# An encoder layer in split float32r: a quarter of the low parts made by an adding transfer instead of VectorE

## The chip, the cores and the metric

The kernel runs on one core of one Trainium2 chip. The metric is the device time of one execution in microseconds (us), the median of several runs. The engines are named as the profile names them: PE (TensorE), PEld (its weight loads), DVE (VectorE), ACT (ScalarE), POOL (GpSimd) and SP (SyncE, which here only issues transfers).

## What is computed

One encoder layer on 256 tokens of width 2048, all in float32:

```python
x = x + 0.5 * swiglu(rms_norm(x, ffn1_norm), ffn1_w_gu, ffn1_w_down)    # 2048 -> 2 x 5632 -> 2048
h = rms_norm(x, mix_norm); p = h @ w_in                                 # 2048 -> 4608
x = x + concat(gqa_axial(p), diff_attention(p)) @ w_out                 # 8 + 4 heads, 256 x 256 scores
x = x + 0.5 * swiglu(rms_norm(x, ffn2_norm), ffn2_w_gu, ffn2_w_down)
x = rms_norm(x, out_norm)
```

Nearly all of the arithmetic is in the products with the weights, about 338 MB of them, each read once from HBM.

## The kernel before

Tokens lie on the partitions of every result. To get float32 accuracy from float32r products, each operand is split into a high part (a cast to float32r) and a low part (the operand minus its high part), and each product is three matmuls: high x high, high x low, low x high (lines 191, 192 and 193). The high part of a weight is made by ACT (line 125, tile `whi`), the low part by DVE (line 126, tile `wlo`), both from the loaded tile `raw`.

`mm_block` is the loop around every weight product. It works on a block of up to 1024 columns of the weights and walks down its rows in **steps**. A step c takes 256 rows, that is two row blocks of 128, k = 2c and 2c + 1. One transfer issued by SP loads both (line 172, 1024 KB, into one of three `raw` buffers), ACT casts the two row blocks, DVE makes the two low parts, and PE runs 2 banks x 2 token tiles x 2 row blocks x 3 = 24 matmuls of 128 x 512. `whi` and `wlo` have four buffers each, which is two steps' worth. The last step of a block is followed by an evacuation on DVE or ACT.

Three stages follow each other: the first feed-forward half step (about 0 to 730 us), the mixer (about 730 to 1050 us) and the second feed-forward half step. In the mixer DVE has more to do beside the low parts: QK norms (`ssq`, line 406), rotary, the 32 x 32 transposes of the heads (`kTa`, `qT`, `kTb`, line 432) and the softmax (`mx`, `nb`, `ri`, `e`, lines 452 to 488). POOL computes a part of the rotary there (`tmp`, line 421) and the reciprocal roots (`rs`, line 100). In the very first block of the kernel x and x.T are loaded beside the weights (`x`, `raw_x`), and the first two steps are loaded in quarters (line 169). In the very last block, `t_major`, the work is ordered by token tile.

The order of the instructions on each engine is chosen by a scheduler at build time, which goes by its own simulated times; a tile pool makes the writer of a buffer wait for that buffer's readers. So the raw buffer of step c takes the load of step c + 3, and SP waits for the last reader of it.

Of the kernel before, what the change touches and what calls it, by code (L numbers as in the profile page):

```python
# [13 lines left out]
F32 = mybir.dt.float32  # L14
F32R = mybir.dt.float32r
AF = mybir.ActivationFunctionType
ALU = mybir.AluOpType
# [24 lines left out]
def encoder_layer(ctx: ExitStack, tc: tile.TileContext, a: dict, out: bass.AP):  # L42
    """Tokens lie on the partitions of x and of every product's result; the operands of the weight
    products are split into two float32r parts that add up to them exactly, and each product runs as
    hi*hi + hi*lo + lo*hi on the tensor engine."""
# [5 lines left out]
    wlo_p = ctx.enter_context(tc.tile_pool(name="wlo", bufs=4))  # L51
# [14 lines left out]
    def load_gain(n):  # L66
        """a norm's gain with the features on partitions, [128, 16]"""
        g = const.tile([P, NK], F32, name=f"gain_{n}")
        nc.gpsimd.dma_start(g, a[n])
        return g  # L70
# [3 lines left out]
    # The tensor engine's clock rises while the first loads are under way.  # L74
# [6 lines left out]
    # Stages of side work (transposes, attention) wait here, to be issued between the steps of a  # L81
    # weight product once their operands are long there.
# [13 lines left out]
    def rsqrt_mean(dst, ssq, n, width):  # L96
        """dst = (ssq / n + EPS) ** -0.5"""
# [6 lines left out]
    class Norm:  # L104
        """rstd of x, gathered by pieces of the columns, in their order."""
# [21 lines left out]

    def new_xT():
        return (xt_p.tile([P, NK, T], F32R, name="xT_hi"), xt_p.tile([P, NK, T], F32R, name="xT_lo"))

    def fill_xT(xT, g, ks):
        """xT[:, k, :] = (x * gain).T for two k at a time."""
# [16 lines left out]
    def late_load(dst, src):  # L149
        """a load for later, kept from running ahead of the first weights"""  # L150
# [3 lines left out]
    def mm_block(lhs, nk, w, row0, col0, width, evac, before=None, after=None, slots=1, t_major=None):  # L154
        """out[t][:, b * 512:...] = lhs.T @ w[row0:row0 + nk * 128, col0:col0 + width], by banks."""
# [4 lines left out]
        parts = {}  # L160

        def load(c):
# [12 lines left out]
            for j in range(2):  # L175
                own = t_major is not None and c > 0
                hi = (t_major if own else whi_p).tile([P, WB], F32R, name="whi")
                lo = (t_major if own else wlo_p).tile([P, WB], F32R, name="wlo")
                for b in range(0, width, fine):
                    splits.append(split(hi[:, b:b + fine], lo[:, b:b + fine], raw[:, j, b:b + fine]))  # L180
                parts[2 * c + j] = (hi, lo)

        def mm(b, t, ks, c0=0, c1=512):
            if ks[0] == 0:
                ps[b, t] = ps_mm.tile([P, 512], F32, name="psm")
            o = ps[b, t][:, c0:c1]
            for k in ks:
# [3 lines left out]
                nc.tensor.matmul(o, xh, wh, start=k == 0, stop=False)  # L191
                nc.tensor.matmul(o, xh, wl, start=False, stop=False)  # L192
                nc.tensor.matmul(o, xl, wh, start=False, stop=k == nk - 1)  # L193
# [478 lines left out]
```

## Time and profile before

| what | value |
|---|---|
| median of 3 runs | 1803.1 us (1802.27 to 1803.56) |
| span of the profiled execution | 1797.4 us, 5.7 us below the median; the page lists no other time for it |
| PE busy | 1772.5 us (99% of the span), 7860 matmuls |
| DVE busy | 1191.6 us (66%) |
| ACT busy | 808.2 us (45%) |
| POOL busy | 47.3 us (3%) |
| DMA | 341.03 MB, mean 190 GB/s; SP's queue 56.4% of 16 engines' span |
| granted PE clock | 0.998 of full speed, mean |

The span runs from the first to the last instruction. An engine's busy share is a mean over the three stages. A wait is put down to what came last before the waiting engine went on. DMA share is the mean busy share of the core's 16 DMA engines.

### The profile page before, as it was taken

What the parts mean: (1) busy time and instruction counts of PE and PEld (TensorE: products, weight loads), DVE (VectorE), ACT (ScalarE), POOL (GpSimd) and SP (SyncE); (2) the same over time, 40 slices, a digit from 0 to 9 for tenths busy, and PEclk for the clock granted to TensorE, in tenths of its full rate; (3) what the DMA queues carried; (4) which work ended last, traced back from release to release, by engine and by line L of the source; (5) the groups of instructions that cost most, each with busy time, mean ns of one, the idle gap of its engine ahead of it and who ended that gap; (6) DMA issues with size and microseconds to landing.
All of it is one profiled execution on the core that took longest, in us unless ns stands there. A gap on an engine that the chain in (4) does not pass through costs nothing.

```text
span 1797.4 us, 20551 instructions
## 1 busy us (share of the span) xinstructions
PE 1772.5 (99%) x7860; PEld 1462.0 (81%) x7860; DVE 1191.6 (66%) x1763; ACT 808.2 (45%) x1073; POOL 47.3 (3%) x75
## 2 busy tenths in 40 slices
PE   9999999999999999998999999999999999999998
PEld 7888888888888888877778888888888888888886
DVE  6475855845846767779987664566746746647676
ACT  6444443443443444745555354343443443443444
POOL 0000000000000000112110000000000000000000
PEclk9999999999999999999999999999999999999999
DMA  9555565565655475654345455565555555655573
GB/s 344 195 187 190 186 210 188 187 200 190 197 191 198 148 234 184 195 184 163 113 146 188 166 185 187 191 206 188 189 193 200 190 190 195 201 187 188 154 242 120
DMA packets 97667, 341.03 MB, mean 190 GB/s; under 512 B 6384, under 2 KB 7840, under 8 KB 97440
## 3 DMA queue, kind: packets, MB, share of 16 engines
q1 hardware_dynamic: 96752, 338.39, 56.4%
q8 instruction: 61, 1.00, 0.2%
q10 hardware_dynamic: 720, 1.31, 0.2%
q14 instruction: 38, 0.31, 0.1%
q0 software_dynamic: 96, 0.02, 0.0%
HBM read 337.60 MB, written 2.10 MB: 189 GB/s over the span
## 4 chain that ended last, share of the span: by engine, by line
PE 91%; DVE 6%; issue 1%; DMA 1%; ACT 1%; POOL 0%; POOLq 0%; ACTq 0%
PE psm L192 30%; PE psm L193 30%; PE psm L191 30%; DVE wlo L126 2%; DVE qT L432 1%; DVE kTb L432 1%; POOL tmp L421 0%; PE psx L138 0%; DMA raw<-in_ffn_w_down 0%; PE psx L535 0%; PE psx L515 0%; DVE kTa L432 0%; DVE ssq L406 0%; PE psx L500 0%; DVE tmp L414 0%
## 5 line engine op out<-in xcount | busy, mean ns | idle before, releaser
L126 DVE TENSOR_TENSOR wlo<-raw,whi 128x1024 fp32r<-128x1024 f32 (+1 forms) x676 | 758.4, 1152 | 550.7 <-ACT whi L125 546.6
L125 ACT CAST whi<-raw 128x1024 fp32r<-128x1024 f32 (+1 forms) x676 | 649.4, 996 | 842.4 <-PE psm L193 750.9
L192 PE MATMUL psm<-wlo,xT_hi 128*128 128x512 f32 x1696 | 659.9, 392 | 8.7 <-DVE wlo L126 8.5
L193 PE MATMUL psm<-whi,xT_lo 128*128 128x512 f32 x1696 | 657.3, 390 | 0.0
L191 PE MATMUL psm<-whi,xT_hi 128*128 128x512 f32 x1696 | 585.9, 390 | 1.4 <-ACT xT_hi L317 1.4
L192 PEld LDWEIGHTS psm<-wlo,xT_hi 128*128 128x128 f32 x1696 | 318.7, 188 | 78.2 <-DVE wlo L126 12.4
L191 PEld LDWEIGHTS psm<-whi,xT_hi 128*128 128x128 f32 x1696 | 318.3, 188 | 68.4 <-ACT xT_hi L317 2.3
L193 PEld LDWEIGHTS psm<-whi,xT_lo 128*128 128x128 f32 x1696 | 318.8, 188 | 65.7
L192 PE MATMUL psm<-wlo,hT_hi 128*128 128x512 f32 x836 | 323.1, 389 | 0.0
L193 PE MATMUL psm<-whi,hT_lo 128*128 128x512 f32 x836 | 322.8, 389 | 0.0
L191 PE MATMUL psm<-whi,hT_hi 128*128 128x512 f32 x836 | 295.2, 389 | 0.0
L192 PEld LDWEIGHTS psm<-wlo,hT_hi 128*128 128x128 f32 x836 | 157.0, 188 | 32.4 <-DVE wlo L126 0.4
L193 PEld LDWEIGHTS psm<-whi,hT_lo 128*128 128x128 f32 x836 | 157.0, 188 | 32.1
L191 PEld LDWEIGHTS psm<-whi,hT_hi 128*128 128x128 f32 x836 | 157.0, 188 | 32.1
L270 DVE STREAM_TRANSPOSE turned<-h 32x256 f32<-32x256 f32 (+1 forms) x384 | 158.8, 413 | 6.5
L228 DVE SCALAR_TENSOR_TENSOR x<-psm,x 128x512 f32<-128x512 f32 (+1 forms) x113 | 72.1, 679 | 5.7 <-PE psm L193 5.2
L122 POOL TENSOR_TENSOR rstd<-ms,minus_half 128x1 f32<-128x1 f32 x8 | 4.6, 575 | 1498.7 <-DVE ms L121 1498.7
L125 ACT CAST hT_hi<-turned 128x512 fp32r<-128x512 f32 x44 | 24.1, 617 | 38.5 <-DVE turned L270 38.5
L432 DVE STREAM_TRANSPOSE qT<-tmp 32x128 f32<-32x128 f32 x128 | 38.7, 302 | 1.7
L242 ACT ACTIVATE sg<-psm,rstd 128x512 f32<-128x512 f32 x44 | 28.4, 687 | 9.5 <-PE psm L193 9.5
L257 DVE SCALAR_TENSOR_TENSOR h<-psm,rstd,sg 128x512 f32<-128x512 f32 x44 | 32.0, 747 | 0.3
L126 DVE TENSOR_TENSOR hT_lo<-turned,hT_hi 128x512 fp32r<-128x512 f32 x44 | 30.0, 686 | 1.4 <-ACT hT_hi L125 1.4
(94 smaller groups left out, 400.7 us busy)
## 6 DMA issues: line engine op xcount, KB each, us to landing
raw<-in_ffn_w_gu SPq DMA_DIRECT2D x158, 1024.0 KB, 4.9
raw<-in_ffn_w_down SPq DMA_DIRECT2D x88, 1024.0 KB, 5.0
raw<-in_w_in SPq DMA_DIRECT2D x32, 1024.0 KB, 5.1
raw<-in_ffn_w_gu SPq DMA_DIRECT2D x32, 512.0 KB, 3.7
raw<-in_w_out SPq DMA_DIRECT2D x16, 1024.0 KB, 4.9
raw<-in_w_in SPq DMA_DIRECT2D x8, 512.0 KB, 3.8
raw<-in_ffn_w_gu SPq DMA_DIRECT2D x8, 256.0 KB, 5.3
x<-in_x SPq DMA_DIRECT2D x8, 256.0 KB, 9.6
```

The lines of the kernel that those rows point to most:

```text
L122: nc.gpsimd.tensor_tensor(self.rstd[t], ms, minus_half[:, :1], op=ALU.pow)
L125: nc.scalar.copy(hi, src)
L126: return nc.vector.tensor_tensor(lo, src, f32(hi), op=ALU.subtract)
L191: nc.tensor.matmul(o, xh, wh, start=k == 0, stop=False)
L192: nc.tensor.matmul(o, xh, wl, start=False, stop=False)
L193: nc.tensor.matmul(o, xl, wh, start=False, stop=k == nk - 1)
L228: nc.vector.scalar_tensor_tensor(x[t][:, s], ps[:, c0:c1], scale, x[t][:, s], op0=ALU.mult, op1=ALU.add)
L242: nc.scalar.activation(sg[t][:, b * 512:(b + 1) * 512], ps, AF.Silu, scale=norm.rstd[t][:, 0:1])
L257: nc.vector.scalar_tensor_tensor(h[t][:, s], ps, norm.rstd[t][:, 0:1], sg[t][:, s], op0=ALU.mult, op1=ALU.mult)
L270: nc.vector.transpose(turned[q * B32:(q + 1) * B32, :nk, t * P + i * B32:t * P + (i + 1) * B32], src[:, :, q, :])
L432: nc.vector.transpose(dst[q * B32:(q + 1) * B32, :, rows], src[:, :, q, :])
```

## The change

In every block but the last one, every row block with k % 4 = 1 (in the first block of the kernel from k = 4 on) gets its low part in another way: ACT casts the high part as before, ACT also writes the negative of the high part into a new tile `wadd`, and a transfer issued by POOL adds `raw` to it within SBUF. The row block's matmul high x low is taken out of its own step and issued in the next one, as the last product on the same PSUM bank. `wlo` goes from four buffers to three, `wadd` gets two. To find the room, the rotary tables of the mixer get a pool of their own, which is closed before the mixer's working tiles are allocated.

The diff, without changed comments and the moved pools of the mixer:

```diff
-    wlo_p = ctx.enter_context(tc.tile_pool(name="wlo", bufs=4))
+    wlo_p = ctx.enter_context(tc.tile_pool(name="wlo", bufs=3))
+    wadd_p = ctx.enter_context(tc.tile_pool(name="wadd", bufs=2))
...
+    def split_by_dma(hi, lo, src):
+        nc.scalar.copy(hi, src)
+        nc.scalar.activation(lo, f32(hi), AF.Copy, scale=-1.0)
+        return nc.gpsimd.dma_start(f32(lo), src, accum_op=ALU.add)
...
+        later = {}
+        def added(k):
+            return t_major is None and k % 4 == 1 and (before is None or k >= 4)
...
-                lo = (t_major if own else wlo_p).tile([P, WB], F32R, name="wlo")
-                for b in range(0, width, fine):
-                    splits.append(split(hi[:, b:b + fine], lo[:, b:b + fine], raw[:, j, b:b + fine]))
+                if added(2 * c + j):
+                    lo = wadd_p.tile([P, WB], F32R, name="wadd")
+                    split_by_dma(hi[:, :width], lo[:, :width], raw[:, j, :width])
+                else:
+                    lo = (t_major if own else wlo_p).tile([P, WB], F32R, name="wlo")
+                    for b in range(0, width, fine):
+                        splits.append(split(hi[:, b:b + fine], lo[:, b:b + fine], raw[:, j, b:b + fine]))
...
-                nc.tensor.matmul(o, xh, wh, start=k == 0, stop=False)
-                nc.tensor.matmul(o, xh, wl, start=False, stop=False)
-                nc.tensor.matmul(o, xl, wh, start=False, stop=k == nk - 1)
+                terms.append((xh, wh))
+                if added(k):
+                    later.setdefault((b, t), []).append((xh, wl))
+                else:
+                    terms.append((xh, wl))
+                terms.append((xl, wh))
+            if not added(ks[-1]):
+                terms += later.pop((b, t), [])
+            for i, (u, v) in enumerate(terms):
+                nc.tensor.matmul(o, u, v, start=ks[0] == 0 and i == 0,
+                                 stop=ks[-1] == nk - 1 and i == len(terms) - 1)
```

In the changed program ACT writes 166 `wadd` tiles (20 of them 512 wide, the others 1024), POOL issues 166 adding transfers, and DVE makes 510 weight low parts where it made 676.

The change moves instructions. On **PE**, in a gate block of the first half step, the matmuls of an odd step of the changed program (its first row block is `whi_2679`, its second `whi_2683`; `wadd_2647` belongs to the step before), from the fifth matmul of the step on:

```order
L217 MATMUL psm_2651<-wlo_2680,xT_hi_113 128x512
L217 MATMUL psm_2651<-whi_2679,xT_lo_114 128x512
L217 MATMUL psm_2651<-whi_2683,xT_hi_113 128x512
L217 MATMUL psm_2657<-wlo_2680,xT_hi_113 128x512
L217 MATMUL psm_2657<-whi_2679,xT_lo_114 128x512
L217 MATMUL psm_2657<-whi_2683,xT_hi_113 128x512
L217 MATMUL psm_2663<-wlo_2680,xT_hi_113 128x512
L217 MATMUL psm_2663<-whi_2679,xT_lo_114 128x512
L217 MATMUL psm_2663<-whi_2683,xT_hi_113 128x512
L217 MATMUL psm_2651<-wlo_2684,xT_hi_113 128x512
L217 MATMUL psm_2651<-whi_2683,xT_lo_114 128x512
L217 MATMUL psm_2651<-wadd_2647,xT_hi_113 128x512
```

Four matmuls on `whi_2679` stand ahead of these, so the first product with `wadd` is the 16th of the step. An even step now has 20 matmuls (none on its `wadd`) and an odd step 28, where each had 24.

On **SP**, in an up block of the first half step, the loads with what they wait for (DMAHW: an earlier load's semaphore; DVE: the low parts made from that buffer; DMASW: a transfer issued by POOL). Before:

```order
L172 DMA raw_1787<-in_ffn1_w_gu 128x2x1024 [waits DMAHW5_49,DVE_49]
L172 DMA raw_1823<-in_ffn1_w_gu 128x2x1024 [waits DMAHW6_49,DVE_49]
L172 DMA raw_1859<-in_ffn1_w_gu 128x2x1024 [waits DMAHW7_49,DVE_49]
L172 DMA raw_1893<-in_ffn1_w_gu 128x2x1024 [waits DMAHW0_49,DVE_49]
L172 DMA raw_1927<-in_ffn1_w_gu 128x2x1024 [waits DMAHW1_49,DVE_49]
```

and with the change:

```order
L184 DMA raw_1810<-in_ffn1_w_gu 128x2x1024 [waits DMAHW5_49,DVE_49]
L184 DMA raw_1843<-in_ffn1_w_gu 128x2x1024 [waits DMASW6_49,DMAHW6_49,DVE_49,Activation_49]
L184 DMA raw_1883<-in_ffn1_w_gu 128x2x1024 [waits DMAHW7_49,DVE_49]
L184 DMA raw_1914<-in_ffn1_w_gu 128x2x1024 [waits DMASW7_49,DMAHW0_49,DVE_49,Activation_49]
L184 DMA raw_1952<-in_ffn1_w_gu 128x2x1024 [waits DMAHW1_49,DVE_49]
```

Every second load now waits for an adding transfer to land.

On **POOL**, in the mixer where the queries of group A are worked on. Before:

```order
L421 TENSOR_TENSOR tmp<-q_sb,gs_aq_5351 128x4x32 x4
L100 TENSOR_TENSOR rs_5950<-ms,minus_half 128x4
L421 TENSOR_TENSOR tmp<-q_sb,gs_aq_5355 128x4x32 x4
L100 TENSOR_TENSOR rs_5982<-ms,minus_half 128x4
L421 TENSOR_TENSOR tmp<-q_sb,gs_aq_5351 128x4x32 x4
L100 TENSOR_TENSOR rs_6014<-ms,minus_half 128x4
```

and with the change:

```order
L453 TENSOR_TENSOR tmp<-q_sb,gs_aq_5423 128x4x32 x4
L101 TENSOR_TENSOR rs_6031<-ms,minus_half 128x4
L453 TENSOR_TENSOR tmp<-q_sb,gs_aq_5427 128x4x32 x4
L101 TENSOR_TENSOR rs_6064<-ms,minus_half 128x4
L133 DMA wadd<-raw 128x1024
L453 TENSOR_TENSOR tmp<-q_sb,gs_aq_5423 128x4x32 x4
L101 TENSOR_TENSOR rs_6097<-ms,minus_half 128x4
L133 DMA wadd<-raw 128x1024
```

The adding transfers stand in POOL's order between the rotary products and the roots.

## Rows read from the trace of the kernel before

**Rows 1.** The page, part 1: busy us, share of the span, instructions.

```profile
PE 1772.5 (99%) x7860; PEld 1462.0 (81%) x7860; DVE 1191.6 (66%) x1763; ACT 808.2 (45%) x1073; POOL 47.3 (3%) x75
```

**Rows 2.** Windows, the two feed-forward stages: stretch, length, busy (instructions), PEclk, DMA share, GB/s.

```profile
100.00:700.00 600.00, 600.00 (x2648) 496.51 (x2647) 386.64 (x498) 248.05 (x277) 0.00 (x0) 1.00 0.59 195
1100.00:1740.00 640.00, 640.00 (x2825) 530.12 (x2824) 400.63 (x501) 265.48 (x294) 0.00 (x0) 1.00 0.58 193
```

**Rows 3.** Windows, the mixer; order of engines: PE, PEld, DVE, ACT, POOL.

```profile
750.00:960.00 210.00, 196.31 (x863) 159.07 (x862) 182.05 (x411) 113.79 (x206) 37.41 (x54) 0.99 0.47 159
...
800.00:850.00 50.00, 44.69 (x195) 35.78 (x195) 48.10 (x111) 25.14 (x51) 11.11 (x16) 1.00 0.44 148
850.00:900.00 50.00, 46.00 (x209) 36.96 (x209) 47.28 (x115) 30.41 (x61) 9.02 (x12) 1.00 0.39 132
```

**Rows 4.** Waits of PE, 740 to 960 us: us in total, times, longest.

```profile
PE psm L192 <- DVE wlo L126: 8.5, 5, 2.4
PE psx L515 <- DVE qT L432: 2.0, 1, 2.0
PE psx L500 <- ACT e L456: 1.7, 2, 1.0
PE psx L480 <- DVE qT L432: 1.0, 1, 1.0
PE psx L480 <- ACT pT L467: 0.4, 1, 0.4
```

**Rows 5.** Groups of DVE, 750 to 960 us: busy, mean ns, idle before.

```profile
L126 DVE TENSOR_TENSOR wlo<-raw,whi 128x1024 fp32r<-128x1024 f32 x64 | 76.4, 1220 | 19.7 <-ACT whi L125 19.4
L432 DVE STREAM_TRANSPOSE qT<-tmp 32x128 f32<-32x128 f32 x128 | 38.7, 302 | 1.7
```

**Rows 6.** Timeline of ACT, 104 to 121 us: start, us, what, idle before.

```profile
103.73 2.01 ACT L125 CAST whi<-raw 128x1024 fp32r<-128x1024 f32 x2 [3.43 <-PE psm L193]
109.17 2.01 ACT L125 CAST whi<-raw 128x1024 fp32r<-128x1024 f32 x2 [3.43 <-PE psm L193]
```

**Rows 7.** Groups of ACT, whole span.

```profile
L125 ACT CAST whi<-raw 128x1024 fp32r<-128x1024 f32 x588 | 595.3, 1052 | 793.8 <-PE psm L193 740.2 <-issue 35.4 <-DMA raw<-in_ffn_w_down 7.4
```

**Rows 8.** Line 172, the weight loads, 100 to 700 us.

```profile
L172 SPq DMA_DIRECT2D raw<-in_ffn_w_gu x75: 367/368/368, 102.0 to 647.1; - x75
...
DMA to landing us min/median/max: 3.5/4.9/7.9
```

**Rows 9.** Line 69, the only transfers that POOL issues.

```profile
L69 POOL DMA_DIRECT2D gain_ffn_norm<-in_ffn_norm x2: 537/636/736, 1.3 to 2.6; - x2
...
DMA to landing us min/median/max: 4.3/5.1/5.1
```

**Rows 10.** Windows, the first block of the kernel.

```profile
16.00:28.00 12.00, 12.00 (x54) 9.94 (x54) 8.75 (x12) 9.99 (x20) 0.00 (x0) 1.00 1.04 397
28.00:40.00 12.00, 12.00 (x54) 9.93 (x54) 7.88 (x13) 9.30 (x18) 1.29 (x2) 1.00 1.02 384
```

**Rows 11.** Timeline of ACT, the first block: casts of steps 5 and 7.

```profile
27.10 2.21 ACT L125 CAST whi<-raw 128x1024 fp32r<-128x1024 f32 x2 [1.03 <-DMA raw<-in_ffn_w_gu]
...
37.09 1.05 ACT L125 CAST whi<-raw 128x1024 fp32r<-128x1024 f32 x1 [0.31 <-PE psm L193]
```

**Rows 12.** The chain that ended last, the first block: start, us, what.

```profile
17.33 0.91 PE psm L191 x4
```

**Rows 13.** The chain that ended last, the last block.

```profile
1764.69 7.17 DMA raw<-in_ffn_w_down
...
1771.88 1.06 ACT whi L125
```

**Rows 14.** Timeline of PE, its last matmul.

```profile
1788.55 0.28 PE L193 MATMUL psm<-whi,hT_lo 128*128 128x256 f32 x1
```

**Rows 15.** Waits of POOL, 750 to 960 us.

```profile
POOL tmp L421 <- DVE ssq L406: 26.0, 7, 10.0
POOL rs L100 <- DVE ms L99: 21.9, 9, 5.1
```

More of the change, by code (lines that the diff above doesn't have):

```diff
@@ L186, in mm @@
             o = ps[b, t][:, c0:c1]
+            terms = []
             for k in ks:
@@ L342, in encoder_layer @@
         ffn(xT, norm1, a["ffn1_w_gu"], a["ffn1_w_down"], start_mix, before=load_xT, after=load_x)
-    with tc.tile_pool(name="mix", bufs=1) as mp, tc.tile_pool(name="mixw", bufs=2) as mw:
+    with ExitStack() as mixer:
+        mp = mixer.enter_context(tc.tile_pool(name="mix", bufs=1))
+        tables = ExitStack()
+        tp = tables.enter_context(tc.tile_pool(name="tables", bufs=1))
         def bcast(src, n):
-            t_ = mw.tile([P, n], F32, name=f"bcast{n}", bufs=1 if n > HD else 2)
+            t_ = tp.tile([P, n], F32, name=f"bcast{n}", bufs=1 if n > HD else 2)
             late_load(t_, src.partition_broadcast(P))
@@ L355, in encoder_layer @@
             for t in range(NT):
-                cs = mw.tile([P, 2, nrot], F32, name=f"cs{t}", bufs=1)
+                cs = tp.tile([P, 2, nrot], F32, name=f"cs{t}", bufs=1)
                 late_load(cs, a[f"rope_{grp}"][t * P:(t + 1) * P])
@@ L360, in encoder_layer @@
                 g = bcast(a[f"{grp}_{n}_norm"], HD)
-                gsw = mw.tile([P, nrot], F32, name="gsw", bufs=1)
+                gsw = tp.tile([P, nrot], F32, name="gsw", bufs=1)
                 gv = g[:, :nrot].rearrange("p (g s d) -> p g s d", s=2, d=hs)
@@ L389, in encoder_layer @@
         nc.vector.tensor_scalar(lam, lam, LAMBDA_INIT, None, op0=ALU.add)
+        tables.close()
+        mw = mixer.enter_context(tc.tile_pool(name="mixw", bufs=2))
         qTa = mp.tile([P, 8, T], F32, name="qT")
```

## Prediction
> **What bounds the kernel now.** I read the page's busy shares first: PE is busy for 1772.5 of 1797.4 us [rows 1], so at most 25 us of the span can come from PE's idle time, wherever it is. The windows by stage tell where it is not. In the two feed-forward stages PE is busy for 600.00 of 600.00 us and 640.00 of 640.00 us [rows 2]; DVE is busy there for 64% and 63%, so a lighter DVE gives nothing back. In the mixer, from 750 to 960 us, PE is busy for 196.31 of 210 us, and 13.7 us are lost; DVE is at 182.05 of 210, and at 48.10 and 47.28 of 50 in the two stretches where PE loses most [rows 3]. The waits of PE say what it waited for: 8.5 us in five waits for a low part from DVE, 3.0 us for the transposes from DVE, 2.1 us for ACT's `e` and `pT`, together 13.6 us [rows 4]. So the change can gain in the mixer alone, and at most 13.7 us there. The rest of PE's idle time lies at the start and behind the last matmul, where no low part is made by a transfer.
>
> **The unit of time.** Casts start every 109.17 - 103.73 = 5.44 us [rows 6], which is one step of 24 matmuls, so 0.2267 us for each. The number of matmuls does not change. An even step of 20 takes 4.53 us now, an odd one of 28 takes 6.35 us, a pair 10.88 us as before.
>
> **Removed: 166 low parts on DVE.** In the mixer's 210 us there are 64 of them at 1.19 us of busy time each (76.4 / 64 [rows 5]); 16 go, 19.0 us of DVE. Its busy time falls from 182 to 163 us. The five waits for low parts are at most 2.4 us long and DVE saves 1.19 us in each 10.88 us ahead of them, so most of them should close. They will not close wholly: a run of 16 transposes holds DVE for 16 x 0.302 = 4.8 us [rows 5], and the one low part that DVE still makes in an even step, or the two of an odd step, may stand behind it. I take 7.0 of the 8.5 us, half of the 3.0 us of transposes and half of the 2.1 us of ACT: 9.5 us gained. The ends are 0 and 13.7. I take a value nearer the upper end because the 19.0 us freed exceed the 13.7 us lost.
>
> **Added: the negative on ACT.** No row shows it. The nearest is the cast of the same shape, 1.052 us [rows 7]. ACT is busy for 248 of 600 us in the feed-forward [rows 2] and 113.79 of 210 us in the mixer [rows 3]; 1.05 us for each 10.88 us takes that to 51% and 64%. It is hidden behind ACT's own wait of 3.43 us for PE in each step [rows 6]. Were that cover gone it would cost 166 x 1.05 = 174 us, but nothing else uses it. A bound below nothing is excluded, since ACT gets no work less.
>
> **Added: the transfer.** POOL's issue takes 0.54 to 0.74 us [rows 9], and POOL is idle in the feed-forward. The even step's casts begin as the odd step before it begins (call it 0), end at 2.0 us, the negative at 3.1 us, the issue at 3.8 us. The first product with `wadd` is the 16th of the next odd step, so it comes at 6.35 + 4.53 + 15 x 0.2267 = 14.3 us. That leaves 10.5 us from issue to landing. POOL's 8 KB transfers took up to 5.1 us [rows 9], a 1024 KB load took 4.9 us, at most 7.9 [rows 8]. I take 4.9 to 7.9 us; hidden, price 0, with at least 2.6 us over.
>
> **Moved: the release of raw.** Every second load now waits for the landing, at 3.8 + 4.9 = 8.7 to 3.8 + 7.9 = 11.7 us, instead of some 3.5 us. It lands 4.9 to 7.9 us later, at 13.6 to 19.6 us. Its cast can begin when PE frees the high parts, at 6.35 + 4.53 + 6.35 = 17.2 us, and PE wants the result 4.53 us later. In the worst case the cast ends at 20.7 us, 1.0 us ahead of its use. Price 0. SP holds only loads, so nothing else queues behind that wait except in the first block.
>
> **The 16 DMA engines.** Loads take a share of 0.58 to 0.59 [rows 2]: 0.58 x 5.44 = 3.16 us of all sixteen per 1024 KB, 6.3 us per pair of steps, and 4.6 us stay free. No row shows an adding transfer. As a plain copy its 512 KB would take 1.58 us; counted as two passes over the data, 3.16 us. Either fits, with a share of 0.73 or 0.87. The Trainium skill has a rule that speaks against the change here (Collectives: The Full Stack, The bandwidth ceiling: the fold count and why AG ≠ RS ≠ AR): an add in the transfer engines needs two source reads and so runs at half the rate of a copy. By that rule the dearer of my two prices would hold and the sum would be the same; no run so far shows it.
>
> **The first block.** Until 40 us the DMA engines are full, 1.04 and 1.02 [rows 10]. Three adds bring 4.7 to 9.5 us of their time. Step 5 was cast at 27.10 us, step 7 at 37.09 us [rows 11]; PE needs them at 33.65 and 44.53 us (step 2 begins at 17.33 us [rows 12], 5.44 us each), so 5.5 and 6.4 us of slack lie behind a cast. With the change an odd step begins four matmuls, 0.9 us, earlier, which leaves 4.6 and 5.5 us. The loads of x stand behind the waiting weight load in SP's queue. I take 1.0 us of loss, between 0 and 5.
>
> **The last block.** The last load waits for an add of the block before it. It left at 1764.69 us and its cast began at 1771.88 us [rows 13]. The last matmul, half as wide as the others, ends at 1788.83 us [rows 14]. Ahead of that end lie 24 half-wide matmuls (2.7 us at half of 0.2267) and 24 full ones (5.4 us), so PE comes to that step at about 1780.7 us. An add that lands 4 to 7 us later than the low part did stays within that. Price 0. Three `wlo` buffers instead of four carry three low parts per pair of steps instead of four, so they last as long: price 0. The tables' pool moves addresses only: price 0.
>
> **The sum.** 9.5 us gained and 1.0 us lost make 8.5 us. Against the profiled span of 1797.4 us that is 1788.9; the median stands 5.7 us above that span, so **1794.6 us**. This case reaches from 1803.1 - 13.7 = 1789.4 to about 1799 (half of the gain, and 2 to 3 us lost in the first block). I give it 0.64.
>
> **Rivals.**
> - *The waits only change their name.* POOL works in order. In the mixer its adds stand behind `rs` and `tmp`, which waited 21.9 us in nine and 26.0 us in seven waits for DVE, the longest 10.0 us [rows 15]. An add held up so long uses up the 10.5 us that it has. DVE's runs of transposes stay as long as they were. Then PE waits for `wadd` where it waited for `wlo`: 1800 to 1805 us. For it speaks that order, against it that most of those 16 waits had no low part behind them. Chance 0.17.
> - *The DMA engines become the bound: slower.* Its place is the feed-forward, where PE has no slack. It decides as soon as an add takes more than the 4.6 us that sixteen engines have free per pair, 2.9 times the copy's 1.58 us. Some 122 full pairs lie there (166 adds less 28 in the mixer and 16 narrow ones). At 5.0 us each pair grows by 0.4 us, 1803 - 9 + 49 = 1843 us; at four copies' price, 6.3 us, it would be 2000 us. For it: nothing in the trace bounds an add from above. Against it: two passes need only 3.2 us. Chance 0.13.
> - *The first block costs more than the mixer gives.* If each of the three adds delays a load by its landing of about 8 us, the slack of 4.6 and 5.5 us is passed by 2.5 to 3.4 us each time: 7.5 to 10 us in three, and with a gain of only 2 to 4 us the end is 1807 to 1811 us. Chance 0.06.
> - That the change does not do what it says is ruled out by the changed program's order, which holds 166 adds.
>
> **How the numbers follow.** The runs lie within 1.3 us of each other; I take 0.2%, 3.6 us, as what can be told from no change. Faster: 0.64 from the forecast and 0.03 of the first rival, 0.67. Same: 0.13 of the first rival and 0.01 of the third, 0.14. Slower: 0.01, 0.13 and 0.05, 0.19. The range runs from 1788 (the whole idle time, and the runs' scatter) to 1806 (the first rival's end); the second rival and most of the third, 0.18, lie above.
>
> **What would show it.** Right: PE busy through both feed-forward stages as before; in the mixer PE's waits for low parts from about 8.5 us down to 1 or 2, DVE at about 163 of 210 us; adds landing within 10 us; a DMA share of 0.7 to 0.9. Wrong: gaps of PE in the feed-forward behind `wadd`, or casts that wait for `raw` (the second rival); waits of PE on `wadd` between 750 and 960 us (the first); gaps before 45 us (the third).

## The result, and the profile after

The changed kernel takes 1858.5 us (median; 1857.35 to 1860.8) where the kernel before takes 1803.1: a ratio of 1.0316, 95% interval 1.0303 to 1.0329. That is slower, on the side that had a chance of 0.19, and far outside the range of 1788 to 1806. Ratios here and below are estimates from fast runs with their intervals, not quotients of the medians. The profiled execution has a span of 1855.6 us, 58.2 more than before.

The busy shares of the page, which answer to [rows 1]:

```profile
PE 1796.6 (97%) x7860; PEld 1465.6 (79%) x7860; DVE 1017.5 (55%) x1597; ACT 966.3 (52%) x1239; POOL 191.9 (10%) x241
```

DVE has 174 us less to do, as the change meant. PE runs the same 7860 matmuls, is busy 24 us longer and idle 34 us longer. Busy time can grow without more work: from 100 to 600 us, at a granted clock of 1.00, 2170 matmuls keep PE busy for 494.84 us, 0.2280 us each, where [rows 2] gives 600.00 / 2648 = 0.2266. That is some 3 us lost inside the busy time, beside 5.1 us of PE's waits in that stretch.

**Where the time went.** The windows view counts PE's instructions from the start to any time T. The kernel before reached the same count earlier, and the difference is how far the changed kernel is behind at T. Two such windows of the changed kernel (stretch, length, PE busy (instructions), PEclk, DMA share, GB/s):

```profile
0.00:600.00 600.00, 592.24 (x2584) 1.00 0.81 245
0.00:960.00 960.00, 921.51 (x3994) 0.99 0.77 228
```

and the windows of the kernel before that hold the same counts:

```profile
0.00:590.00 590.00, 587.39 (x2584) 1.00 0.61 205
0.00:918.00 918.00, 903.64 (x3994) 1.00 0.58 194
```

So the changed kernel is 10 us behind at 600 us and 42 at 960. Read in this way, in steps of 0.5 us:

| stretch of the changed kernel | what runs there | lost, us |
|---|---|---|
| 0 to 100 | the first block | 1.5 |
| 100 to 600 | first feed-forward stage, blocks of 1024 columns | 8.5 |
| 600 to 700 | with its blocks of 512 columns (casts of 512 from 624.93 to 674.07 us) | 11.5 |
| 700 to 760 | turn to the mixer | 9.5 |
| 760 to 960 | mixer | 11.0 |
| 960 to 1680 | rest of the mixer, second feed-forward stage at 1024 columns | -0.5 |
| 1680 to 1800 | with its blocks of 512 columns (from 1716.70 us) | 11.5 |
| 1800 to 1840 | last block | 5.5 |

The mixer, from which the gain was to come, loses time, and the feed-forward stages lose more. The second feed-forward stage runs the same program at 1024 columns as the first and loses nothing. The 8.5 us of the first are not lost evenly either: the changed kernel is 1.5 us behind at 180 us, 4.0 at 260 and at 320, 6.0 at 340 and at 400, 9.0 at 440 and at 580, and 10.0 at 600.

**The first feed-forward stage.** The waits of ACT for the loads tell the two stages apart. From 100 to 600 us (engine, tile and line, released by: us in total, times, longest):

```profile
ACT whi L126 <- DMA raw<-in_ffn_w_gu: 100.7, 35, 6.4
ACT whi L126 <- PE psm L217: 88.7, 36, 8.6
ACT whi L126 <- DMA raw<-in_ffn_w_down: 59.7, 18, 6.9
```

and from 1120 to 1540 us:

```profile
ACT whi L126 <- PE psm L217: 197.0, 75, 3.3
...
ACT whi L126 <- DMA raw<-in_ffn_w_gu: 1.9, 1, 1.9
```

In the second stage the casts wait for PE, as in [rows 6]: the loads are ahead. In the first, more than half of them wait for the load. The adds' time from issue to landing differs in the same way; from 100 to 600 us, then from 1120 to 1540 us:

```profile
L133 POOL DMA_DIRECT2D wadd<-raw x45: 855/855/857, 102.5 to 593.2; - x45
...
DMA to landing us min/median/max: 4.5/8.0/11.2
L133 POOL DMA_DIRECT2D wadd<-raw x38: 862/862/887, 1130.8 to 1533.3; - x38
DMA to landing us min/median/max: 4.5/4.7/6.1
```

The chain of waits shows the loop at the place where the first of these losses falls (start, us, what):

```profile
190.08 10.74 DMA wadd<-raw
...
201.43 10.01 DMA raw<-in_ffn_w_down
...
211.50 3.40 issue
...
214.92 9.42 DMA wadd<-raw
```

SP at that place:

```profile
200.97 0.88 SPq L184 DMA_DIRECT2D raw<-in_ffn_w_down  x2
```

An add is issued at 190.08 and lands at 200.8 us. SP has waited for it, and now issues two loads at once: the one that needed the buffer, and the one behind it, whose own buffer had been free since DVE's low parts from it ended at 198.6 us. The second is the even step that holds the next add of this loop. It lands after 10.0 us (the first after 5.8), the casts and the negative take 3.4 us, and the next add goes out at 214.92. From add to add 24.84 us have passed in a loop that has four steps, 4 x 5.44 = 21.76 us, to close. This turn is one of the longest. Adds of two such loops alternate, so two intervals between adds make a turn: the 45 adds from 102.5 to 593.2 us make turns of 490.7 / 22 = 22.3 us in the mean, the 38 of the second stage, from 1130.8 to 1533.3 us, turns of 402.5 / 18.5 = 21.76 us. Slow adds alone do not cost time at once: from 260 to 320 us they land after 9.5 us in the median, and nothing is lost. In blocks of 512 columns the four steps last 10.88 us, and one turn of the loop, from load to load, takes 670.56 - 657.10 = 13.46 us:

```profile
657.10 4.66 DMA raw<-in_ffn_w_gu
...
670.56 7.72 DMA raw<-in_ffn_w_down
```

**The turn to the mixer.** The loads of the rotary tables stand in SP's queue behind two weight loads that an add, landing at 719.9 us, let go together:

```profile
720.03 0.88 SPq L184 DMA_DIRECT2D raw<-in_ffn_w_down  x2
...
722.23 0.44 SPq L159 DMA_DIRECT2D bcast<-in_a_q_norm  x1
```

This table lands after 10.3 us, where it took 3.5 in the kernel before. DVE stands still for it, with the evacuation of PE's banks (`x`) behind:

```profile
722.40 0.69 DVE L253 SCALAR_TENSOR_TENSOR x<-psm,x 128x512 f32<-128x512 f32 x1
732.66 0.30 DVE L394 COPY gsw<-bcast 128x64 f32<-128x64 f32 x2 [9.57 <-DMA bcast<-in_a_q_norm]
...
733.27 0.68 DVE L253 SCALAR_TENSOR_TENSOR x<-psm,x 128x512 f32<-128x512 f32 x1
```

**The mixer.** PE's waits from 760 to 960 us, which answer to [rows 4]:

```profile
PE psm L217 <- DVE wlo L127: 5.4, 3, 3.6
PE psx L512 <- ACT e L488: 4.2, 1, 4.2
PE psx L496 <- ACT e L488: 3.7, 1, 3.7
PE psx L512 <- DVE qT L464: 1.6, 1, 1.6
PE psm L217 <- DMA wadd<-raw: 1.5, 1, 1.5
```

Before, ten waits were at most 2.4 us long; now two for the exponentials last 4.2 and 3.7 us, and one for a low part 3.6. DVE's timeline shows where one comes from. The score maximum `mx` is there at 857.16 us; its negative `nb`, for which ACT's exponential waits, is 0.17 us of work, and it stands behind 16 transposes and two other operations:

```profile
856.48 0.68 DVE L484 TENSOR_REDUCE mx<-psx 128x2 f32<-128x512 f32 x1
857.08 0.68 DVE L446 TENSOR_TENSOR tmp<-q_sb,gc_aq 128x512 f32<-128x512 f32 x1
857.68 2.50 DVE L464 STREAM_TRANSPOSE qT<-tmp 32x128 f32<-32x128 f32 x8
860.21 0.69 DVE L438 TENSOR_REDUCE ssq<-tmp 128x4 f32<-128x512 f32 x1
860.93 2.52 DVE L464 STREAM_TRANSPOSE qT<-tmp 32x128 f32<-32x128 f32 x8
863.48 0.17 DVE L486 TENSOR_SCALAR nb<-mx 128x2 f32<-128x2 f32 x1
```

This gap costs twice. PE's windows of 2 us around it:

```profile
862.00:864.00 2.00, 0.00 (x0) 0.66 0.79 147
864.00:866.00 2.00, 1.24 (x3) 0.50 0.11 14
866.00:868.00 2.00, 2.00 (x6) 0.50 0.86 250
868.00:870.00 2.00, 2.00 (x7) 0.64 0.94 309
```

The granted clock falls to 0.50, the 1.2 GHz level, in the gap and stays there until about 869 us: some 2.4 us of matmul time are lost on top of the wait. Between 720 and 980 us the changed kernel has four stretches at half clock, of 3 to 7 us, and the kernel before one (928 to 934 us). In single executions these vary: e4_tables below, which takes the kernel before's time, has three of some 3.5 us.

### The profile page after: what moved, and what is told of

It is laid out like the page before. It is cut to its first block, busy times and chain, and to the rows that moved or that the text cites. A ratio compares the mean times of both kernels' runs of the same rounds, so it can differ in the third digit from the quotient of the medians.

```text
span 1855.6 us, 21329 instructions
## 1 busy us (share of the span) xinstructions
PE 1796.6 (97%) x7860; PEld 1465.6 (79%) x7860; DVE 1017.5 (55%) x1597; ACT 966.3 (52%) x1239; POOL 191.9 (10%) x241
## 3 DMA queue, kind: packets, MB, share of 16 engines
q0 software_dynamic: 24000, 81.82, 22.8%
## 4 chain that ended last, share of the span: by engine, by line
PE 60%; DMA 24%; DVE 7%; issue 6%; ACT 2%; SPq 0%; POOL 0%; POOLq 0%; ACTq 0%; DVEq 0%
PE psm L217 58%; DMA wadd<-raw 10%; DMA raw<-in_ffn_w_gu 7%; DMA raw<-in_ffn_w_down 5%; DVE wlo L127 2%; DMA raw<-in_w_in 2%; DVE qT L464 1%; DVE kTb L464 1%; ACT whi L126 1%; DMA bcast<-in_a_q_norm 1%; DVE x L253 1%; PE psx L567 0%; SPq L184 0%; DMA cs<-in_rope_b 0%; PE psx L532 0%
## 5 line engine op out<-in xcount | busy, mean ns | idle before, releaser
L127 DVE TENSOR_TENSOR wlo<-raw,whi 128x1024 fp32r<-128x1024 f32 (+1 forms) x510 | 575.9, 1152 | 715.6 <-ACT whi L126 714.3
L217 PE MATMUL psm<-wlo,xT_hi 128*128 128x512 f32 x1276 | 502.9, 395 | 5.7 <-DVE wlo L127 5.4
L133 POOL DMA_DIRECT2D wadd<-raw x166 | 143.3, 864 | 1536.7 <-ACT wadd L132 1147.9
L217 PEld LDWEIGHTS psm<-wlo,xT_hi 128*128 128x128 f32 x1276 | 240.9, 189 | 63.9 <-DVE wlo L127 14.4
L217 PE MATMUL psm<-wlo,hT_hi 128*128 128x512 f32 (+1 forms) x632 | 247.3, 392 | 4.3 <-DVE wlo L127 4.1
L132 ACT ACTIVATE wadd<-whi 128x1024 fp32r<-128x1024 f32 (+1 forms) x166 | 167.6, 1009 | 4.8
L217 PE MATMUL psm<-wadd,xT_hi 128*128 128x512 f32 x420 | 162.3, 391 | 3.6 <-DMA wadd<-raw 3.6
L217 PEld LDWEIGHTS psm<-wlo,hT_hi 128*128 128x128 f32 x632 | 119.5, 189 | 31.0 <-DVE wlo L127 6.9
L217 PEld LDWEIGHTS psm<-wadd,xT_hi 128*128 128x128 f32 x420 | 78.6, 188 | 22.2 <-DMA wadd<-raw 6.0
L217 PE MATMUL psm<-wadd,hT_hi 128*128 128x512 f32 x204 | 80.0, 394 | 4.1 <-DMA wadd<-raw 4.0
```

The costliest lines, as they stand in the source:

```text
L127: return nc.vector.tensor_tensor(lo, src, f32(hi), op=ALU.subtract)
L132: nc.scalar.activation(lo, f32(hi), AF.Copy, scale=-1.0)
L133: return nc.gpsimd.dma_start(f32(lo), src, accum_op=ALU.add)
L217: nc.tensor.matmul(o, u, v, start=ks[0] == 0 and i == 0, stop=ks[-1] == nk - 1 and i == len(terms) - 1)
```

## The experiments

Each edit is against the changed kernel unless it says otherwise. Ratios are to the kernel before, measured on the same chip with the run, with their 95% intervals; the medians of the kernel before lay between 1800.4 and 1802.3 us there.

### Do held loads cost the time, or the shared DMA engines?

**e1_hbm.** The add reads its rows from HBM again:

```diff
-        return nc.gpsimd.dma_start(f32(lo), src, accum_op=ALU.add)
+        return nc.gpsimd.dma_start(lo, again.bitcast(F32R), accum_op=ALU.add)
...
-                    split_by_dma(hi[:, :width], lo[:, :width], raw[:, j, :width])
+                    split_by_dma(hi[:, :width], lo[:, :width], raw[:, j, :width],
+                                 w[r + j * P:r + (j + 1) * P, col0:col0 + width])
```

> The adding transfer takes its rows from HBM a second time instead of from the loaded buffer, so no load waits for an add; the adds stay as many and as large, and HBM reads grow by 82 MB. Theory HOLD (each second load waits for the landing of an add, and the load behind it in SP's queue waits with it): the feed-forward stages run as before the change except for waits on the added low part itself; of the 55 us lost some 30 come back, 1820 to 1835 us. Rival CONTENTION (the loads are late because the adds share the 16 DMA engines with them): nothing comes back, since there is no less to move: 1855 us or more.

Measured: 1817.6 us, ratio 1.0080 (1.0063 to 1.0098). 41 of the 55 us come back, although the DMA engines now have more to do. The two feed-forward windows, to be read beside [rows 2]:

```profile
100.00:700.00 600.00, 598.49 (x2640) 495.08 (x2639) 325.09 (x437) 304.70 (x333) 50.58 (x59) 1.00 0.86 241
1100.00:1740.00 640.00, 640.00 (x2823) 529.41 (x2822) 328.65 (x420) 325.53 (x355) 53.52 (x62) 1.00 0.86 238
```

PE is nearly full again (598.49 of 600 us, and 640.00 of 640) at a DMA share of 0.86 and with adds that take 7.5 us to land in the median. CONTENTION falls as the cause of these 41 us: neither the share nor the landing time by itself stops PE there. It is the hold on the loaded buffer. HOLD stands; its range began 2 us above the result.

**e3_wide.** No adds in blocks of 512 columns: `added` asks for `width == WB` too.

> Blocks of 512 columns make all their low parts on DVE again; the 146 full-width adds stay. Theory HOLD: the 512-wide blocks, whose steps last 2.72 us, lose about 10 us at the end of the first and 9 us at the end of the second feed-forward stage; these come back: 1836 to 1842 us. Rival CONTENTION: a 512-wide add moves half the bytes in half the time, so its share of the loss goes by bytes (20 half adds of 156 full ones), 55 x 10 / 156 = 3.5 us: 1855 us.

Measured: 1832.1 us, ratio 1.0166 (1.0150 to 1.0182). 26 us come back, above HOLD's 16 to 22 and far from the 3.5 by bytes. One add in eight held nearly half of the loss; the loop has half the time there (10.88 us, and the turn above took 13.46).

**e5_noadd.** `split_by_dma` ends after the negative; the transfer is left out.

> The adding transfer is left out, so the low part of these row blocks is the negative of the high part alone; ACT's second pass, the later product, the buffers and the moved pools stay. HOLD and CONTENTION both say that the feed-forward stages are then free of waits. What is over 1803 us is owed to the moved pools, the order or the mixer: the forecast before the change gave 1790 to 1795 us; theory POOLS (the moved tables cost 8 us at the mixer's start by themselves): 1800 to 1805 us.

Measured: 1803.6 us, ratio 1.0006 (0.9997 to 1.0015). At the points read up to 760 us it is no more than 0.5 us away from the kernel before. In the mixer its profiled execution loses 3 us instead of gaining 9.5, and by the ratio's interval a gain is no more than some 0.5 us. So the forecast's gain fails by itself, without any transfer.

**e4_tables.** The kernel before, with the tables in a pool of their own that closes ahead of the working tiles' pool:

```diff
-    with tc.tile_pool(name="mix", bufs=1) as mp, tc.tile_pool(name="mixw", bufs=2) as mw:
+    with ExitStack() as mixer:
+        mp = mixer.enter_context(tc.tile_pool(name="mix", bufs=1))
+        tables = ExitStack()
+        tp = tables.enter_context(tc.tile_pool(name="tables", bufs=1))
...
+        tables.close()
+        mw = mixer.enter_context(tc.tile_pool(name="mixw", bufs=2))
```

> The kernel before with the rotary tables in a pool of their own and nothing else changed. Theory POOLS: DVE stands still for the tables' load at the start of the mixer as in the changed kernel (9.6 us), and 5 to 8 us are lost: 1808 to 1811 us. Rival: the late tables follow from late weight loads, not from the pools: 1803 us, no change.

Measured: 1804.1 us, ratio 1.0004 (0.9995 to 1.0014): no change. The pools cost nothing, which fits the other theory: the tables came late because of the weight loads. This rules out POOLS, whose numbers e5_noadd had met by chance.

### Why does less work on DVE gain nothing in the mixer?

PE's waits in e5_noadd from 740 to 960 us, where DVE is busy for 164.27 of 210 us (750 to 960) instead of 182.05 [rows 3]:

```profile
PE psx L512 <- ACT e L488: 4.2, 1, 4.2
PE psx L496 <- ACT e L488: 3.9, 1, 3.9
PE psm L217 <- DVE wlo L127: 3.1, 3, 1.4
PE psx L547 <- DVE qT L464: 1.8, 1, 1.8
```

They sum to 13.0 us where [rows 4] sum to 13.6. The waits for low parts did fall from 8.5 to 3.1 us, as forecast; in their place stand two long ones for `e`, with half clock behind each.

**e6_nb_before, e8_nb_noadd, e7_nb_hbm_wide.** One line, in the kernel before, in e5_noadd and in e9_hbm_wide:

```diff
-            nc.vector.tensor_scalar(nb, mx, -SCALE, None, op0=ALU.mult)
+            nc.scalar.activation(nb, mx, AF.Copy, scale=-SCALE)
```

**e9_hbm_wide** is e1_hbm without adds in blocks of 512 columns.

> The kernel before, with the negative maximum of the softmax (nb) made by ACT instead of DVE and nothing else. Theory ORDER (in the mixer PE waits for exponentials because nb stands behind runs of transposes in DVE's queue): before the change these waits were 1.7 us in two, so 1800 to 1802.5 us, hardly to be told from no change.

> As e5_noadd (the adding transfer left out, so that part of the low part is missing), with nb on ACT. Theory ORDER: PE's two waits for e of 4.2 and 3.9 us and the half clock of some 6.5 us behind each (3.3 us lost each) go: 1803.6 - 8.1 - 6.6 = 1789 us, to 1793 us if part stays. Rival AMOUNT (DVE is simply too busy there, and another wait takes the place): 1799 to 1804 us.

> As e1_hbm (the adds take their rows from HBM), without adds in blocks of 512 columns. Theory HOLD: with the hold gone, the narrow blocks cost only what the added low part itself comes late, 2 to 4 us: 1813 to 1816 us. Rival CONTENTION: by bytes, 15 x 10 / 156 = 1 us: 1816.5 us.

> As e9_hbm_wide with nb on ACT; computes the full result. Theory ORDER: 8 to 15 us less than e9_hbm_wide, 1799 to 1806 us, which would be level with the kernel before. Rival AMOUNT: no change to e9_hbm_wide, 1813 to 1816 us.

Measured: e6_nb_before 1806.9 us, 1.0025 (1.0015 to 1.0035), slower and above ORDER's 1800 to 1802.5. e8_nb_noadd 1797.7, 0.9984 (0.9973 to 0.9994). e9_hbm_wide 1811.6, 1.0059 (1.0044 to 1.0074), 0.2% under e1_hbm by the ratios, 3.8 us, within HOLD's 2 to 4; but the intervals overlap, so this run does not decide. e7_nb_hbm_wide 1807.6, 1.0038 (1.0023 to 1.0053), 0.2% under e9_hbm_wide, with intervals that overlap too.

In e8_nb_noadd the waits for `e` are gone from the list, and others have grown (740 to 960 us):

```profile
PE psm L217 <- DVE wlo L127: 7.4, 5, 3.4
PE psx L547 <- DVE qT L464: 2.7, 1, 2.7
```

So ORDER fits the cause of those waits and is wrong about their price: by the ratios about 4 us came back in each of the two instead of 8 to 15, while other waits grew. AMOUNT, with no change, is wrong for e8_nb_noadd, whose interval lies clear of e5_noadd's; for e7_nb_hbm_wide the intervals do not decide. In the kernel before the same line made PE's waits for low parts 12.4 us instead of 8.5. These runs fit the reading that what PE loses in the mixer is set by which work stands in front of which on DVE, and that an edit deals that anew. That is argued: no run changes DVE's order and nothing else.

### Where and how does the hold act?

**e10_queue.** POOL issues the loads of the odd steps:

```diff
-                loads.append(nc.sync.dma_start(
+                odd = c % 2 == 1 and slots == 1 and before is None and t_major is None
+                loads.append((nc.gpsimd if odd else nc.sync).dma_start(
```

> As the changed kernel, but in the feed-forward stages (not in the first and the last block) POOL issues the loads of the odd steps, which wait for an add; SP keeps the even steps' loads, which then stand behind no such wait. HOLD BEHIND (what is late is above all the load that stands behind the waiting one in SP's queue): the gaps of the first feed-forward stage go and most of those of the 512-wide blocks: 1825 to 1840 us. HOLD SELF (only the load that waits itself comes late): 1853 to 1861 us, no change.

Measured: 1983.8 us, ratio 1.0937 (1.0860 to 1.1015). Neither; the edit made a new queue of the same kind. POOL's timeline shows it:

```profile
307.23 0.72 POOL L185 DMA_DIRECT2D raw<-in_ffn_w_gu  x1 [8.39 <-DVE wlo L127]
309.60 0.87 POOL L133 DMA_DIRECT2D wadd<-raw  x1 [1.65 <-ACT wadd L132]
```

POOL waits for a low part before it can issue the load, and the add stands behind that. The run does not tell BEHIND from SELF. That the load behind is the one that counts is read from the chain above (the second of two loads issued from 200.97 us on ends in the next add), not shown by a run.

**e2_slim.** The add covers 64 columns: `dma_start(f32(lo)[:, :64], src[:, :64], ...)`.

> As the changed kernel, but each adding transfer covers 64 of its 1024 (or 512) columns; the rest of the low part stays the negative of the high part. All waits and orders stay; the bytes of the adds fall by 94%. HOLD by latency: a small transfer lands in some 3 us or more where the adds took 6; the full-width blocks run freely, the 512-wide ones (loop of four steps 10.9 us; issue 0.9 + landing 3 + load 4.5 + casts 2 = 10.4 us) lose 0 to 4 us: 1808 to 1818 us. CONTENTION: as without adds, 1803 to 1806 us.

Measured: 1809.2 us, ratio 1.0035 (1.0024 to 1.0047), in HOLD's range. The adds land in 2.2 us, and at 700 us the kernel is 2 us behind; 5 us of the rest are lost between 760 and 960 us. With the wait in place but short, nearly all of the loss is gone. Together with e1_hbm, where the adds land slowly and no load waits for them, this says that it takes both, the hold and a slow landing: the hold costs where issue, landing, load and casts together exceed four steps.

**e11_mixer_only.** `added` asks for `slots > 1 and width == WB`: 24 adds, in the mixer alone.

> As the changed kernel, with adds only in the full-width blocks of the mixer, 24 of 166. HOLD: the feed-forward stages run as before; in the mixer PE waits 4.2 and 3.9 us for the exponentials with half clock behind, as in e5_noadd, and a few us more for late loads: 1804 to 1812 us. If the first forecast's gain exists at all, it shows here: 1794 us.

Measured: 1804.8 us, ratio 1.0017 (1.0006 to 1.0027). That is in HOLD's range: no gain, and waits of 4.2 and 3.7 us for `e`. The change is not worth anything even where it was meant to help and where the other stages have no add.

**e12_pool_mixer.** The same 24 row blocks, with the low part subtracted by POOL:

```diff
-        nc.scalar.activation(lo, f32(hi), AF.Copy, scale=-1.0)
-        return nc.gpsimd.dma_start(f32(lo), src, accum_op=ALU.add)
+        return nc.gpsimd.tensor_tensor(lo, src, f32(hi), op=ALU.subtract)
```

> As e11_mixer_only, but POOL subtracts the high part itself instead of issuing an add, and ACT writes no negative; computes the full result. If the relief of DVE in the mixer is worth something once no transfer is in it: 1795 to 1800 us. Theory ORDER (the waits for e stay as in e5_noadd): 1802 to 1806 us; POOL's subtraction holding up its rotary work or DVE: above 1806 us.

Measured: 1816.5 us, ratio 1.0069 (1.0053 to 1.0086), above all forecasts but the last. PE's waits for low parts are 9.2 us between 740 and 980 us, and DVE's own low parts are longer, 1344 ns in the mean where e11_mixer_only has 1226 (both 750 to 960 us). The group in e12_pool_mixer (busy, mean ns | idle before it):

```profile
L127 DVE TENSOR_TENSOR wlo<-raw,whi 128x1024 fp32r<-128x1024 f32 x43 | 57.5, 1344 | 25.2 <-ACT whi L126 24.9
```

and in e11_mixer_only:

```profile
L127 DVE TENSOR_TENSOR wlo<-raw,whi 128x1024 fp32r<-128x1024 f32 x46 | 56.2, 1226 | 30.8 <-ACT whi L126 30.5
```

The Trainium skill has a rule for this (SBUF — State Buffer, Who interferes with whom): a DVE instruction with two inputs in SBUF contends with a GpSimd instruction that reads SBUF. The trace agrees in sign, with 118 ns a piece; no run here separates it from other causes.

### Why only the first feed-forward stage, and what of the ends?

**e13_nofirst** is e3_wide without adds in the first block (`before is None`); **e14_notails** is e13_nofirst without adds in blocks of two steps (`nk > 4`).

> As e3_wide (no adds in blocks of 512 columns), and no adds in the first block of the kernel either. Theory REGIME (once the loads have fallen behind, in the busy first block, the loop add - two loads - cast - add of four steps takes as long as the four steps and never catches up, so the first feed-forward stage pays all along): that stage runs free as the second one did, some 8 us less than e3_wide: 1822 to 1826 us. Rival: the loop falls behind by itself within a stage whatever its start: 1830 to 1834 us, as e3_wide.

> As e13_nofirst, and no adds in the short blocks (two steps each) that end a feed-forward stage either. In e3_wide these went with 10 us at the mixer's start, where the loads of its tables wait in SP's queue behind held loads and DVE stands still for them, and with one wait of PE of 7.9 us and half clock behind it in the last block, whose load waits for an add. Theory HOLD AT THE ENDS: both go: 1803 to 1812 us. Rival: the ends are late because of the adds before them in any case: within 4 us of e13_nofirst.

Measured: e13_nofirst 1830.2 us, 1.0162 (1.0147 to 1.0177). That is in the rival's range: the first block is not what sets the regime, and the stage is 8 us behind at 600 us as in e3_wide. But the trace shows two ways of running all the same. Waits of ACT in e13_nofirst from 60 to 130 us:

```profile
ACT whi L126 <- PE psm L217: 35.5, 14, 3.3
ACT whi L126 <- DMA raw<-in_ffn_w_gu: 1.1, 1, 1.1
```

and from 139 to 600 us:

```profile
ACT whi L126 <- DMA raw<-in_ffn_w_gu: 132.3, 43, 6.2
...
ACT whi L126 <- PE psm L217: 14.4, 11, 2.2
```

The adds land in 5.1 us in the first stretch and in 9.2 us in the second (medians). What lies between is the end of a gate block: ACT gets four casts of `hT_hi` and the first of four evacuations `sg` ahead of the negative. The add of POOL comes 13.39 us after the one before it instead of 10.88:

```profile
122.83 0.86 POOL L133 DMA_DIRECT2D wadd<-raw  x1 [10.02 <-ACT wadd L132]
136.22 0.86 POOL L133 DMA_DIRECT2D wadd<-raw  x1 [12.53 <-PE psm L217]
```

It takes 6.1 us to land, SP's two loads leave at 142.43 us, and the next add, issued at 144.59, runs into them and lands after 9.0 us. From then on most adds meet the pair of loads that the add before it let go. In the second stage the same disturbance comes at 1220.76 us in this run; that add lands in 4.5 us, the next in 6.4, and the loads stay ahead. So the loop can run for long with adds that land in some 5 us or in some 9, and in the first stage it went over at a delay of 2 to 3 us. Such a delay does not decide by itself, as the second stage shows, and why it tips in one place and not in the other is not settled. In the changed kernel the adds of the second stage get slow only from about 1550 us on, and up to 1680 us that costs nothing.

e14_notails took 1815.6 us, 1.0087 (1.0070 to 1.0104), some 14 us less than e13_nofirst and 3.6 above the theory's range. The wait of 7.9 us in the last block is gone, wholly. Of the loss between 700 and 760 us, 9.0 us in e13_nofirst, 6.5 are left, so half of that theory fell. The table that DVE waits for lands after 6.3 us there and not 3.5, which fits loads that are late from the blocks before as well.

How far behind the kernel before each one is, in us, by the same counts:

| at T, us | changed | e1_hbm | e3_wide | e13_nofirst | e14_notails | e11_mixer_only | e5_noadd |
|---|---|---|---|---|---|---|---|
| 600 | 10.0 | 3.5 | 8.0 | 8.0 | 4.5 | 0.0 | 0.0 |
| 700 | 21.5 | 5.5 | 8.0 | 8.0 | 4.5 | 0.0 | 0.0 |
| 760 | 31.0 | 13.0 | 19.0 | 17.0 | 11.0 | 2.5 | -0.5 |
| 960 | 42.0 | 15.0 | 18.5 | 20.5 | 12.5 | 6.0 | 2.5 |
| 1680 | 41.5 | 16.0 | 19.0 | 20.0 | 12.5 | 6.0 | 2.5 |
| end of span | 58.2 | 19.1 | 31.6 | 30.7 | 13.6 | 5.9 | 3.9 |

Each column is one execution against one of the kernel before, and that one was quick: its span is 1797.4 us, where its spans beside the experiments have medians of 1798.6 to 1800.5. e4_tables, whose runs take as long as the kernel before's, lies 1.5 us behind at 100 us, 5.5 at 960 and 5.4 at the end. So differences of up to some 5 us in this table cannot be told from scatter, those of the first 100 us above all: e12_pool_mixer, which has no add there, is 3.0 us behind at 100.

What e1_hbm still loses (3.5 us at the start, 9 between 640 and 760 us, 3 at the end) was not taken apart; what is left is some 15 us of the 55.

### The later product by itself

**e15_defer.** DVE makes all low parts again; only the later product and the buffers are left of the change. **e16_defer_half** does so for the second row block of every step but a block's last.

```diff
-        nc.scalar.activation(lo, f32(hi), AF.Copy, scale=-1.0)
-        return nc.gpsimd.dma_start(f32(lo), src, accum_op=ALU.add)
+        return nc.vector.tensor_tensor(lo, src, f32(hi), op=ALU.subtract)
```

> As the changed kernel, but the low part of these row blocks is made by DVE as before, in the same tiles, and its product is issued one step later; there is no negative and no transfer. The later product by itself, theory SLACK (PE's 8.5 us of waits for low parts in the mixer come from DVE's runs of transposes; one low part in four gets a step's time more): 1797 to 1801 us. Rival ORDER (DVE's work and order as a whole set these waits, so the others take its place): 1801 to 1806 us.

> As e15_defer, for the second row block of every step (not the last of a block), one low part in two, with three buffers for these and two for the others. SLACK: 1794 to 1799 us, faster than the kernel before. ORDER: 1801 to 1808 us.

Measured: e15_defer 1800.7 us, ratio 0.9996 (0.9987 to 1.0005), no change (the time lies in SLACK's range, but the kernel before took 1800.7 beside it); e16_defer_half 1807.0, 1.0036 (1.0022 to 1.0049), slower, as ORDER had it. PE's waits for low parts are 11.7 and 7.3 us in the two (700 to 980 us), so a step's time more for some of the products does not close them. No kernel that computes the whole result came out faster than the kernel before.

## Why the prediction was wrong

- **What bounds the kernel: right.** PE was full in the feed-forward stages and could only lose there. That was read, but not weighed: with no slack on PE, whatever made a load late would be paid in full, and 166 loads were given something new to wait for.
- **The failed step: "Moved: the release of raw", price 0.** It put the wait at its own load alone and said that "SP holds only loads, so nothing else queues behind that wait except in the first block". The next load queued behind it. With the adds kept and the hold taken away 41 of the 55 us come back (e1_hbm), so this step cost some 41 us and not 0. How it costs is read from the chain: both loads left within 0.88 us, the second took 10.0 us to land, and it carried the next add. The share of the load that waits itself was not told apart (e10_queue does not settle it). The worst case counted one add and one load, each at times of an undisturbed queue (4.9 to 7.9 us); in the first stage the adds took 8.0 us in the median and up to 11.2. The sum had to be made around the loop of four steps: 24.84 us in the turn shown, and 22.3 in the mean of the first stage, against 21.76.
- **The steps were taken as 5.44 us everywhere.** The 20 adds of 512 columns were counted and then left out of the sum. There the loop has 10.88 us and takes 13.46, and the adds, half as large, land in 5.7 us in the median, against 8.0 for the full ones of the stage before. These blocks and what hangs on them cost 26 of the 55 us (e3_wide); most of that is part of the 41 above.
- **The gain of 9.5 us in the mixer: wrong by itself.** Its reason was that the 19.0 us freed exceed the 13.7 us lost. e5_noadd and e11_mixer_only free that work and gain nothing. Fewer low parts did shorten the waits for low parts (8.5 to 3.1 us), but in their place `nb` came to stand behind 16 transposes on DVE, and PE waited for `e`. Two waits of some 4 us there were each followed by a stretch at the 1.2 GHz level. That the order on DVE sets these waits whatever its load is argued, not shown.
- **The last block, price 0: wrong.** In e3_wide the add landed at 1795.53 us, the last load left at 1795.67, and PE waited 7.9 us. Without the add (e14_notails) that wait is gone.
- **The first block, 1.0 us of loss: not contradicted.** The changed kernel is 1.5 us behind at 100 us, but e3_wide, with the same adds there, is 0.5 behind and e4_tables, with none, 1.5; so small a loss does not show in single executions. **The pools: price 0, right** (e4_tables).
- **ACT's negative: right.** It took 1.061 us (1.052 taken), and e5_noadd, which keeps it, loses nothing in the feed-forward stages.
- **The DMA engines' share: right, and beside the point.** The adds' queue took 22.8% of the span of 16 engines, 423 us for 156 full adds' worth of bytes, 2.71 us each: between the copy's 1.58 and the two passes' 3.16 us. The share rose to 0.80 and 0.78 in the feed-forward stages, within the forecast 0.7 to 0.9. The Trainium skill's rule (Collectives: The Full Stack, The bandwidth ceiling: the fold count and why AG ≠ RS ≠ AR), which the page gives for the reducing step of a ring over several ranks, puts an add at half the rate of a copy. The trace has 2.71 / 1.58 = 1.7 in place of 2, and the 1.58 us are of a load; no run here has a plain copy within SBUF.
- **The rivals.** None was this. The second had one of the right places and the right sign by another mechanism: the engines' share stayed at 0.80, and e1_hbm runs at a higher share still. The first, waits that change their name, happened in the mixer, through `e` and not through POOL.

## What to carry to other kernels

When a buffer gets a new reader, follow its release around the whole loop, through the queue that waits for it and what stands behind there, and compare the loop's time with that of the steps it spans, in the smallest blocks too; bandwidth and busy shares say nothing about it. Work taken from an engine is a gain only if the waits it shortens are not dealt anew by the order of what remains: leaving the work out (as in e5_noadd) measures that before the replacement is written.

## What was not expected of the hardware

- A gap of PE of 4.2 us was followed by some 5 us of matmuls at the 1.2 GHz level (864 to 869 us above), and so were gaps of 5.9, 3.7 and 1.8 us in the changed kernel between 720 and 980 us, by 3 to 6 us of them. A gap of 3.6 us before 806.32 us was followed by none, and one of 2.0 us in the kernel before was (928 to 934 us). So the length of a gap alone does not tell what it costs.
- POOL's issue of an add takes 0.86 us where its 8 KB loads took 0.54 to 0.74 [rows 9], and an add of a sixteenth of the bytes lands in 2.2 us in the median (e2_slim) where the full one takes 4.5 us at the least.
- Loads that POOL issues land little later than SP's (8.2 and 7.4 us for the 1024 KB loads of `in_ffn_w_gu` in e10_queue), but share POOL's order with everything else that it issues.
